# Small TensorE products of the token mixers put in another order: by the shape of their operands, two heads side by side

## The chip, the cores and the metric

The kernel runs on one core of a Trainium2 chip. A core has five engines that work side by side and wait for each other through semaphores: PE (TensorE: matrix products, with PEld for the load of the stationary operand), DVE (VectorE), ACT (ScalarE), POOL (GpSimd) and SP (SyncE, which here only issues DMAs). PE takes its work in the order of the program. The metric is the time of one execution on the device, in microseconds.

## What is computed

One step of a two-layer decoder for 16 meta tokens, 512 prompt tokens and 8 x 4 sample tokens (560 columns in all). Each layer adds a mixer and an MLP to the stream, each followed by a norm over 1024 features. The mixer consists of three causal token mixers on the same input: gated linear attention (GLA, 4 heads), Mamba-2 SSD (8 heads, 2 groups) and retention (4 heads). All three are the same recurrence, taken chunk by chunk:

```python
def step(s, inp):                       # one chunk: queries, keys, values, log-decays
    qc, kc, vc, gc = inp
    G = jnp.cumsum(gc, axis=1)
    ...
    o = (jnp.einsum('btsh,bshv->bthv', att, vc)
         + jnp.einsum('bthk,bhkv->bthv', qc * jnp.exp(G), s))
    s_new = (jnp.exp(G_end)[..., None] * s
             + jnp.einsum('bshk,bshv->bhkv', kc * jnp.exp(G_end[:, None] - G), vc))
    return s_new, o
```

An output is the sum of the chunk's own part (weights `att` by values) and of the part of the state that the chunk found (`q` by `s`); the new state adds keys by values. Around the mixers stand large products with the weights: the projections, three gated branch projections, an output projection and an MLP of 4096 hidden features. All results are fp32; the large products run as three products of operands split in two parts.

## The kernel before

The stream is kept feature-major: 128 features in the partitions, tokens in the columns. A **dense** tile is 128 output features for half of the tokens (256 to 288 columns), 24 products of 128x128 weights for an input of 1024 features, in one of three PSUM buffers named `dps`; ACT and DVE split each weight unit into its two parts (`wh`, `wl`) beside them.

The mixers and norms are written as generators, the **background**. `Background.slot` is called four times in each half tile; it adds a credit and, when the credit covers the distance that the last step left (`GAP`), emits the next step in the midst of the dense products. So all orders are fixed when the program is built, and nothing is moved at run time. The queue runs GLA, then SSD, then retention. `together` takes the steps of two generators in turn (one pair's heads beside the next pair's weights). A step may also leave small operations in `bg.soon`, which the following slots emit.

Small products use three PSUM buffers in rotation, `mps` (a bank each), and one of two banks, `sps`. An fp32 product is two passes on PE, so the profile counts two instructions for each.

`heads_gen` (L708) serves GLA and retention, a pair of heads at a time. It runs over four body chunks of 128 tokens (L771). `tokens(c)` (L739) transposes the values of both heads and the keys of a chunk (three transposes), and ACT copies them to `xt`. A chunk then has, for each head, the product of its weights (in `t4a` or `t4b`, all 128 rows) with the values, and onto the same sum the product of the queries (`QS`, 64 rows: head 0 in rows 0 to 63, head 1 in rows 64 to 127) with the state `St` (`S_h` in the profile). Both heads' new states (keys 128 rows, 64 columns) follow. DVE updates the state, ACT copies both outputs over the weights, and the transposes of the next chunk come last on PE.

`ssd` (L1109) takes all eight heads of a chunk at once: after its decays and scores, `out_of(0)` (L1206, L1212) multiplies the weights `E` (tile `t4a`) of heads 0 to 3 with the inputs (`v`), then come the product of `C` with the state `S_s` (64 rows, two groups), the new state (`vh` by `kt`, 64 columns), `out_of(4)` for heads 4 to 7 (L1228) and the transposes of the gate `z` (L1237). `E` of heads 0 to 3 is finished by DVE, that of heads 4 to 7 by POOL, in the step before. DVE then adds up the output `yt` and the state, POOL adds the skip part, DVE multiplies by `z`, ACT squares for the norm; the next chunk's second step transposes the normed output back (`last`).

In the profile most operations show the line of a helper: L304 is any product, L314 any transpose, L317, L326 and L329 are operations of DVE, POOL and ACT. So groups are told apart by their tiles.

Of the kernel before, what the change touches and what calls it, by code (L numbers as in the profile page):

```python
# [31 lines left out]
# weights: buffers for units as loaded, for split ones; units split at a time  # L32
NRAW, NSPLIT, AHEAD = 3, 3, 2
# tiles taken by halves of the tokens: the first ones of the MLP; taken whole before those: w_o, second product of the MLP
FIRST, WHOLE_O, WHOLE_2 = 8, 3, 3
# steps of row scales per slot; products that keep the clock up at the start, beside the first and the last norm
SOON = 3
WARM = 20, 12, 10
# credit of the mixers' and norms' steps per slot, by phase, and the steps' distances
# [9 lines left out]
# ---------------------------------------------------------------- constants of the shapes  # L49
def _const_tables():  # L50
    """Tables that depend on the shapes alone."""
# [66 lines left out]
# ---------------------------------------------------------------- weights: units of [128, 1024], in the order of use  # L118
# [24 lines left out]
def _lay_out(inp):  # L143
    """The inputs in the order in which the chip reads them."""
# [46 lines left out]
def _collect(r):  # L191
    """The chip's outputs in the reference's order and shapes."""
    y = r["y"].transpose(2, 1, 0).reshape(T - NMETA, D)
    cv = r["conv"].transpose(0, 3, 2, 1).reshape(DEPTH, 59, 768)
    cs = cv[:, 3:].reshape(DEPTH, NB, 7, 768)[:, :, 4:7]
    return (np.ascontiguousarray(y[:SEQ].reshape(1, SEQ, D)), np.ascontiguousarray(y[SEQ:].reshape(NB, NS, D)),
            r["state_gla_prompt"], r["state_gla_sample"], r["state_ssm_prompt"], r["state_ssm_sample"],
            np.ascontiguousarray(cv[:, None, 0:3]), np.ascontiguousarray(cs), r["state_ret_prompt"], r["state_ret_sample"])


def bc(ap, axis, n):
    """A view that repeats ap n times along a new axis."""
    u = ap.unsqueeze(axis)
    shape = list(u.shape)
    shape[axis] = n
    return u.to_broadcast(shape)
# [6 lines left out]
class Background:  # L213
    """Steps of the token mixers and norms, dealt out between the dense products."""
# [12 lines left out]
    def one(self):  # L227
        """the next step; it leaves its distance to the one after"""
        while self.q:
            try:  # L230
                self.wait = next(self.q[0]) or 1.0
                return True
            except StopIteration:
                self.q.pop(0)
        self.wait = 0.0
        return False

    def flush(self):
        """what is to come soon, at once"""
        while self.soon:  # L240
            self.soon.pop(0)()
# [19 lines left out]
def together(a, b):  # L261
    """Steps of two generators in turn, until both have ended."""
# [10 lines left out]
def decoder_step_kernel(ctx: ExitStack, tc: tile.TileContext, I, O):  # L273
# [13 lines left out]
    # ---------------------------------------------------------------- buffers  # L287
# [45 lines left out]
    # ---------------------------------------------------------------- input, constants  # L333
# [11 lines left out]
    def warm(n):  # L345
        """products of ones: the tensor engine's clock stays up while it waits"""
# [50 lines left out]
    def rsqrt(y, v, t, n_it=3):  # L397
        """y = v ** -0.5 for v > 0 (t: scratch), in steps"""
# [10 lines left out]
    # ---------------------------------------------------------------- weights, split exactly in two parts  # L409
# [4 lines left out]
    class Stream:  # L414
        """Units in the order of seq: loaded ahead, split ahead; a split unit lives until its last use in the plan."""
# [17 lines left out]
        def room(self, now):  # L433
            """whether no work from plan entry now on reads the next unit's buffer"""
# [8 lines left out]
        def ahead(self, now, most=1 << 30):  # L443
            """split as many units as there are buffers"""
            most = min(len(seq), most, self.n_split + AHEAD)
            while self.n_split < most and self.room(now):
# [4 lines left out]
                if seq[self.n_split][1] == "adt":  # L451
                    # both parts side by side, as one stationary operand
# [19 lines left out]
    # ---------------------------------------------------------------- plan of dense work  # L472
# [3 lines left out]
    def item(keys, emit, again=None, where=((None, 0),)):  # L476
        """work on the units keys, or on those of an earlier item again; where: for each split unit its slab (None: the
        ring) and the first plan entry at which that is free"""
# [13 lines left out]
    def twice(lst, between, side=1, tags=(), since=0):  # L492
        """(keys, emit) per output tile, the first half of all of them before the second; the last units of the first pass
        are the first of the second one, still split. side: so many tiles of a pass begin side by side, where its input
        has just been made. tags: slabs free from plan entry since on, for split units"""
# [25 lines left out]
    def tiles(lst, first=0, tags=(), since=0):  # L521
        """(keys, emit) per output tile; the first ones by halves"""
# [7 lines left out]
    def dense(ws, nk, c, xh, xl, spl, halves, evac, m=128, two=None):  # L530
        """One output tile: a unit of nk row tiles, columns c.. of each; three products per part of the tokens.
        two: the sums of a tile that has two units, by half"""
        w_of = [(a if len(a.shape) == 3 else a.rearrange("p (k c) -> p k c", k=nk))[:, :, c:c + m] for a in ws[0]]
        # products (part of the weights, part of x, row tile): what is made last comes last
# [44 lines left out]
    def silu2(out, p):  # L579
        """out = 2 silu(p)"""  # L580
# [5 lines left out]
    # ---------------------------------------------------------------- norm over features, columns of one half  # L586
    def norm_gen(sums, c0, n, wn, bn, l, last=False, alone=False, first=False):
        """X (pre-norm) -> X, XH, XL (normed); sums: addends of X's sum, of its squares'; last: X, sent out; alone: beside
        nothing else"""
# [3 lines left out]
        # sums over the features, token-major: a chunk of 128 tokens per column  # L593
# [21 lines left out]
        # every partition gets every token's scale and shift  # L615
# [7 lines left out]
        # w (x rs) + (w nm + b)  # L623
# [25 lines left out]
    def x_norm(c0, n, e):  # L649
        """the first norm, of the loaded X; e: engine of the plain sums"""  # L650
# [16 lines left out]
    class Acc:  # L667
        """sums over the features of one half, collected while its tiles are made; apart: the last tile's an addend apart"""
# [6 lines left out]
        def add(self, xo):  # L675
            """one tile more; not beside the other half's norm, which has more need of the engine"""
# [25 lines left out]
    # ---------------------------------------------------------------- linear attention: what GLA and retention share  # L702
    def row_scales(ss, eps, dim):
        """(ss / dim + eps) ** -0.5 and the steps to it"""
# [3 lines left out]
    def heads_gen(hp, v, QS, KH, att, attm, atts, decay, decay_s, l, nm, y, yscal):  # L708
        """Two heads from their weights att [s, h2, c, t]: outputs, states. QS, KH: decayed q, k [128 (h2 k), T]."""
# [6 lines left out]
        # meta and samples, token-major: rows (h2, 32)  # L716
# [22 lines left out]
        def tokens(c):  # L739
# [4 lines left out]
            transpose(p[:, 256:384], KH[:, c0:c0 + 128])  # L744
            vk = T4("xt", [128, 384])
# [3 lines left out]
        vk = tokens(0)  # L749
# [21 lines left out]
        for c in range(4):  # L771
            c0 = NMETA + 128 * c
            po = mps(), mps()
            for h2 in range(2):
                mm(po[h2][:, 0:128], att[:, h2, c], vk[:, sl(h2, 128)], start=True, stop=False)
                mm(po[h2][:, 0:128], QS[sl(h2), c0:c0 + 128], St[sl(h2)], start=False, stop=True)
# [10 lines left out]
            if c < 3:  # L787
                vk = tokens(c + 1)
            yield GAP["hc" + nm[0]]
        sp.dma_start(out=O[f"state_{nm}_prompt"][l, 0, 2 * hp:2 * hp + 2].rearrange("h k v -> (h k) v"), in_=St)  # L790
        # samples
# [53 lines left out]
    # ---------------------------------------------------------------- GLA  # L845
    def gla(l, B):
# [32 lines left out]
        def levels(hp, out):  # L879
# [32 lines left out]
            def small(Xs, Xt, n):  # L912
                """meta and samples; n: place of the level among 8, 4, 2, 1, diagonal"""
# [99 lines left out]
    # ---------------------------------------------------------------- retention  # L1013
# [47 lines left out]
    # ---------------------------------------------------------------- SSD  # L1061
    def ssd_tokens(l, B):
        """the inputs of step sizes and decays, token-major: body chunks 0..3, meta 4, samples 5 (twice, at rows 0 and 32)"""
# [45 lines left out]
    def ssd(l, B):  # L1109
# [3 lines left out]
        # decays from a chunk's start, to its end, over all of it  # L1113
# [30 lines left out]
        def steps(nt, ci, g):  # L1144
            """a of each token, at the columns from that token on"""
# [20 lines left out]
        for c, (c0, nt, ci) in enumerate(chunks):  # L1166
# [43 lines left out]
            if do_o:  # L1210
                po = mps()
                out_of(0)  # L1212
                yt, xd = T4("yt", [128, 512]), T4("sq", [128, 512])
# [13 lines left out]
            if do_o:  # L1227
                out_of(4)  # L1228
# [7 lines left out]
            if do_o:  # L1236
                pz = mps()  # L1237
                for i in range(4):
                    transpose(pz[0:nt, sl(i, 128)], z[:, i, cols])
# [16 lines left out]
        # samples: rows (g, token)  # L1256
# [93 lines left out]
        # columns (i, g, t) of p: feature tile 2 g + i  # L1350
# [4 lines left out]
    # ---------------------------------------------------------------- causal convolution of x, B, C  # L1355
# [39 lines left out]
    # ---------------------------------------------------------------- a layer  # L1395
    def layer(l):
        B = {}
        part = full if l == 0 else ((NMETA, HALF - NMETA), (HALF, T - HALF))
        # the last norm has nothing beside it: the smaller half comes last
# [30 lines left out]
        def split_y(br, nm):  # L1430
            """a mixer's output in two parts, where the one before has been used"""
# [30 lines left out]
        # retention's q, k are rotated one tile later than they are made  # L1462
# [29 lines left out]
        # gates and projections, branch by branch; then the normed x again, for the residual  # L1492
# [54 lines left out]
        # output projection, residual, first norm  # L1547
# [12 lines left out]
        def by_halves(tile_of, whole, wn, bn, tags=(), last=False):  # L1560
            """the last tiles half by half, so that one half's norm runs beside the other half's products"""
# [30 lines left out]
        # MLP in two halves of the hidden features  # L1592
# [87 lines left out]
```

## Time and profile before

| | us |
|---|---|
| median of 3 runs | 2128.74 (2128.52 to 2129.56) |
| span of the profiled execution | 2126.3 |
| PE busy in it | 2087.0 |
| DVE busy | 1119.0 |
| ACT busy | 745.8 |
| POOL busy | 519.8 |
| weights and state read, written | 171.46 MB, 9.67 MB |

The span runs from the first to the last instruction of the profiled execution; no other time of that execution is recorded, so it stands beside the median of the runs. A row of the timeline gives start, length, engine, line, the tile written, the tiles read, for a product the rows*columns of the stationary operand and the shape of the moving one, the number of instructions merged in the row, and in brackets idle time of that engine before it with what ended it. The first mixer's chunks of layer 0 lie at 174 to 280 us of the span, those of SSD at 325 to 400, of retention at 470 to 537; layer 1 has them at 1225 to 1327, 1374 to 1440 and 1512 to 1577.

### The profile page before, as it was taken

To read this page: it belongs to the slowest core of one execution; us is meant where nothing else is said; L and a number is where in the kernel's file an instruction comes from. 1 tells how busy PE (TensorE), PEld (TensorE's weight loads), DVE (VectorE), ACT (ScalarE), POOL (GpSimd) and SP (SyncE) were. 2 spreads that over 40 slices of the span, in tenths; PEclk is the share of its full clock that TensorE was granted. 3 is DMA by queue.
4 is the path that set the end of the run, shared out by engine and by line. 5 is a ranking of instruction groups with operands and counts; after the bars stand their busy time and mean duration, and the time that the engine had idled before them with its cause. 6 is when DMAs were issued, how large, how long until landed. Compare 5 with 4: busy or idle time off the path is not lost.

```text
span 2126.3 us, 39955 instructions
## 1 busy us (share of the span) xinstructions
PE 2087.0 (98%) x16536; PEld 1985.9 (93%) x16536; DVE 1119.0 (53%) x2206; ACT 745.8 (35%) x1373; POOL 519.8 (24%) x670
## 2 busy tenths in 40 slices
PE   8999999999999999999999999999999989999998
PEld 7998899888998999999999989988889989999998
DVE  8576567754556532333375774686544474223335
ACT  5434232222234531243254432322223354214433
POOL 4012114322334310021231121141323342001123
PEclk8999999999999999999999999999999999999999
DMA  4321321232222222222322223213222312222231
GB/s 158 103 80 67 96 86 51 80 92 72 81 91 89 71 89 90 80 90 81 120 101 93 80 71 108 83 54 96 71 72 90 102 68 100 90 90 80 92 128 63
DMA packets 87846, 186.00 MB, mean 87 GB/s; under 512 B 24624, under 2 KB 47216, under 8 KB 87664
## 3 DMA queue, kind: packets, MB, share of 16 engines
q1 hardware_dynamic: 87136, 182.86, 25.8%
q8 instruction: 130, 2.13, 0.4%
q10 hardware_dynamic: 528, 0.59, 0.1%
q14 instruction: 52, 0.43, 0.1%
HBM read 171.46 MB, written 9.67 MB: 85 GB/s over the span
## 4 chain that ended last, share of the span: by engine, by line
PE 86%; DVE 7%; issue 3%; POOL 2%; ACT 1%; DVEq 0%; POOLq 0%; ACTq 0%
PE dps L304 75%; PE mps L304 8%; PE sps L304 2%; PE mps L314 2%; DVE X L326 1%; POOL X L317 1%; DVE wl L317 1%; DVE XL L317 1%; POOL yt L317 0%; DVE xbc L326 0%; DVE S L317 0%; ACT wh L329 0%; POOL S L317 0%; ACT t4a L329 0%; DVE gv L317 0%
## 5 line engine op out<-in xcount | busy, mean ns | idle before, releaser
L304 PE MATMUL dps<-XH,wh 128*128 128x288 f32 (+2 forms) x2784 | 741.4, 296 | 7.1 <-ACT XH L329 6.9
L304 PE MATMUL dps<-XL,wh 128*128 128x288 f32 (+2 forms) x2784 | 727.8, 291 | 2.2 <-DVE XL L317 1.6
L304 PEld LDWEIGHTS dps<-XH,wh 128*128 128x128 f32 x2784 | 525.4, 189 | 21.4 <-ACT XH L329 9.6
L304 PEld LDWEIGHTS dps<-XL,wh 128*128 128x128 f32 x2784 | 524.3, 189 | 6.3 <-DVE XL L317 5.8
L317 DVE TENSOR_TENSOR wl<-raw,wh 128x1024 fp32r<-128x1024 f32 x278 | 345.2, 1243 | 212.3 <-ACT wh L329 197.2
L304 PE MATMUL dps<-XH,wl 128*128 128x288 f32 (+2 forms) x2752 | 429.7, 292 | 0.0
L329 ACT ACTIVATE wh<-raw 128x1024 fp32r<-128x1024 f32 x280 | 292.8, 1047 | 262.7 <-PE dps L304 227.3
L304 PEld LDWEIGHTS dps<-XH,wl 128*128 128x128 f32 x2752 | 380.5, 189 | 4.0 <-issue 2.7
L317 POOL TENSOR_TENSOR S<-th 128x288 f32<-128x288 f32 (+2 forms) x128 | 87.2, 682 | 499.2 <-ACT th L329 496.2
L304 PE MATMUL dps<-gqk,wh 128*128 128x288 f32 (+2 forms) x608 | 142.6, 295 | 1.6 <-ACT gqk L329 1.1
L329 ACT ACTIVATE th<-dps,parcol 128x288 f32<-128x288 f32 (+2 forms) x128 | 62.6, 489 | 187.8 <-PE dps L304 187.8
L304 PE MATMUL dps<-gqk,wl 128*128 128x272 f32 (+2 forms) x496 | 126.8, 292 | 0.0
L304 PE MATMUL dps<-Q,wh 128*128 128x288 f32 (+2 forms) x640 | 116.3, 291 | 0.8 <-ACT Q L329 0.8
L304 PEld LDWEIGHTS dps<-gqk,wh 128*128 128x128 f32 x608 | 104.1, 188 | 5.5 <-ACT gqk L329 2.8
L304 PE MATMUL dps<-gv,wh 128*128 128x288 f32 (+2 forms) x608 | 103.4, 291 | 0.0
L329 ACT ACTIVATE gt<-dps 128x272 f32<-128x272 f32 (+1 forms) x96 | 37.7, 398 | 173.8 <-PE dps L304 168.6
L304 PEld LDWEIGHTS dps<-Q,wh 128*128 128x128 f32 x640 | 96.8, 188 | 1.2 <-ACT Q L329 1.2
L317 DVE TENSOR_TENSOR X<-X,dps 128x288 f32<-128x288 f32 (+2 forms) x64 | 28.2, 441 | 130.1 <-PE dps L304 130.1
L317 POOL TENSOR_TENSOR X<-X,yt 128x288 f32<-128x288 f32 (+2 forms) x77 | 77.3, 1036 | 69.0 <-ACT yt L329 69.0
L304 PEld LDWEIGHTS dps<-gqk,wl 128*128 128x128 f32 x496 | 89.9, 188 | 2.9 <-issue 2.3
L317 POOL TENSOR_TENSOR X<-X,th 128x288 f32<-128x288 f32 (+2 forms) x56 | 47.8, 857 | 174.5 <-DVE th L326 174.4
L304 PEld LDWEIGHTS dps<-gv,wh 128*128 128x128 f32 x608 | 87.1, 188 | 0.4 <-DVE gv L317 0.3
(418 smaller groups left out, 3179.0 us busy)
## 6 DMA issues: line engine op xcount, KB each, us to landing
raw<-in_w SPq DMA_DIRECT2D x304, 512.0 KB, 3.3
craw<-Q SPq DMA_DIRECT2D x32, 70.0 KB, 2.0
S<-in_state_gla SPq DMA_DIRECT2D x8, 256.0 KB, 4.4
out_state_gla_sample<-S SPq DMA_DIRECT2D x8, 256.0 KB, 4.2
S<-in_state_ret SPq DMA_DIRECT2D x8, 256.0 KB, 3.8
out_state_ret_sample<-S SPq DMA_DIRECT2D x8, 256.0 KB, 2.5
S<-in_state_ssm SPq DMA_DIRECT2D x12, 128.0 KB, 3.1
out_state_ssm_sample<-S SPq DMA_DIRECT2D x12, 128.0 KB, 2.7
```

What stands on the lines that cost most here:

```text
L304: pe.matmul(out, lhsT=lhsT, rhs=rhs, start=start, stop=stop)
L314: pe.transpose(out, in_=in_, identity=ident[b:b + p, b:b + p])
L317: e.tensor_tensor(out=out, in0=a, in1=b, op=op)
L326: dve.scalar_tensor_tensor(out=out, in0=a, scalar=s, in1=b, op0=op0, op1=op1)
L329: act.activation(out=out, in_=in_, func=f, **k)
```

## The change

Three things are moved, and no operation is added or left out. In `heads_gen` the transposes of the next chunk go to the front of a chunk (their copy by ACT stays at its end), and the two heads' 128-row products come before their two 64-row products, which then stand next to each other. In `ssd`, `out_of(4)` follows `out_of(0)` at once, and the transposes of `z` follow that, ahead of the state's products. Comments are left out as well.

```diff
@@ heads_gen
-        def tokens(c):
+        def turned(c):
             c0 = NMETA + 128 * c
             p = mps()
             for h2 in range(2):
                 transpose(p[:, sl(h2, 128)], v[:, 2 * hp + h2, c0:c0 + 128])
             transpose(p[:, 256:384], KH[:, c0:c0 + 128])
+            return p
+
+        def tokens(p):
             vk = T4("xt", [128, 384])
             fn(vk, p[:, 0:384], AF.Copy)
             return vk
 
-        vk = tokens(0)
+        vk = tokens(turned(0))
@@
         for c in range(4):
             c0 = NMETA + 128 * c
+            pt = turned(c + 1) if c < 3 else None
             po = mps(), mps()
             for h2 in range(2):
                 mm(po[h2][:, 0:128], att[:, h2, c], vk[:, sl(h2, 128)], start=True, stop=False)
+            for h2 in range(2):
                 mm(po[h2][:, 0:128], QS[sl(h2), c0:c0 + 128], St[sl(h2)], start=False, stop=True)
...
             if c < 3:
-                vk = tokens(c + 1)
+                vk = tokens(pt)
@@ ssd
             if do_o:
                 po = mps()
                 out_of(0)
+                out_of(4)
+                pz = mps()
+                for i in range(4):
+                    transpose(pz[0:nt, sl(i, 128)], z[:, i, cols])
...
             if do_o:
-                out_of(4)
                 tt(dve, yt[0:nt], yt[0:nt] if c else xd[0:nt], po[0:nt], A)
...
             if do_o:
-                pz = mps()
-                for i in range(4):
-                    transpose(pz[0:nt, sl(i, 128)], z[:, i, cols])
                 stt(yt[0:nt], yt[0:nt], 0.5, pz[0:nt], M, M)
```

On PE, at the first chunk of GLA's first pair of heads in layer 0 (tiles: `t4a` the weights, `xt` the transposed values and keys, `X` the queries, `gv` the values; a row here is a product, its shape that of the moving operand):

```order
 L304 MATMUL dps<-XH,wl 128x288 x8
-L304 MATMUL mps<-xt,t4a 128x128
-L304 MATMUL mps<-S_h,X 128x128
-L304 MATMUL mps<-xt,t4a 128x128
-L304 MATMUL mps<-S_h,X 128x128
-L304 MATMUL mps<-xt 64x128 x2
 L314 MATMUL mps<-cst,gv 128x128 x2
 L314 MATMUL mps<-cst,X 128x128
+L304 MATMUL mps<-xt,t4a 128x128 x2
+L304 MATMUL mps<-S_h,X 128x128 x2
+L304 MATMUL mps<-xt 64x128 x2
 L304 MATMUL dps<-XH,wh 128x272
```

The three transposes now stand ahead of the chunk's products, and the products of one kind stand together.

On PE, at the first 128-token chunk of SSD in layer 0 (`v,t4a` the eight heads' weights by inputs, `S_s,xbc` the state product, `vh,kt` the new state, `cst,z` the transposes of the gate):

```order
 L304 MATMUL dps<-XH,wl 128x272 x2
-L304 MATMUL mps<-v,t4a 128x64 x4
+L304 MATMUL mps<-v,t4a 128x64 x8
+L314 MATMUL mps<-cst,z 128x128 x4
 L304 MATMUL sps<-S_s,xbc 128x256 x2
 L304 MATMUL mps<-vh,kt 64x256 x2
-L304 MATMUL mps<-v,t4a 128x64 x4
-L314 MATMUL mps<-cst,z 128x128 x4
 L304 MATMUL dps<-XH,wl 128x272 x6
```

The second four heads and the gate's transposes moved from the end of the block to its front half. The orders of ACT, DVE, POOL and SP are the same as before.

## The prediction, made before the changed kernel ran

> **What bounds the kernel now.** I read the page first: busy times, granted clock, chain.
>
> ```profile
> span 2126.3 us, 39955 instructions
> ...
> PE 2087.0 (98%) x16536; PEld 1985.9 (93%) x16536; DVE 1119.0 (53%) x2206; ACT 745.8 (35%) x1373; POOL 519.8 (24%) x670
> ...
> PEclk8999999999999999999999999999999999999999
> ...
> PE 86%; DVE 7%; issue 3%; POOL 2%; ACT 1%; DVEq 0%; POOLq 0%; ACTq 0%
> ```
>
> TensorE is busy for 98% of the span at full clock and carries 86% of the chain that ended last; the other engines are half idle. So a microsecond less of work on PE, in a stage where PE waits for nobody, is a microsecond off the end, and a new wait of PE is one more. "Busy" hides what matters here, though: it also covers drains between products of different shapes. For those I read the timeline of PE alone around one chunk of the linear-attention heads (start, length, then rows*columns of the stationary operand and the shape of the moving one).
>
> ```profile
> 181.19 0.29 PE L304 MATMUL dps<-XL,wh 128*128 128x288 f32 x1
> 181.32 0.38 PE L304 MATMUL mps<-xt,t4a 128*128 128x128 f32 x2
> 181.63 0.49 PE L304 MATMUL mps<-S_h,X 64*128 64x128 f32 x2
> 182.05 0.49 PE L304 MATMUL mps<-xt,t4a 128*128 128x128 f32 x2
> 182.47 0.49 PE L304 MATMUL mps<-S_h,X 64*128 64x128 f32 x2
> 182.88 0.44 PE L304 MATMUL mps<-xt 128*64 128x128 f32 x4
> 183.25 0.44 PE L314 MATMUL mps<-cst,gv 128*128 128x128 f32 x2
> 183.53 0.27 PE L314 MATMUL mps<-cst,X 128*128 128x128 f32 x1
> 183.55 0.38 PE L304 MATMUL dps<-XH,wh 128*128 128x288 f32 x1
> 183.77 0.29 PE L304 MATMUL dps<-XL,wh 128*128 128x288 f32 x1
> ```
>
> An fp32 product is two passes (x2 for one product). A dense pass follows the one before by 0.13 us (181.19 to 181.32), so the dense pass at 183.55 really begins at 183.77 - 0.13 = 183.64, and the chunk costs 183.64 - 181.32 = **2.32 us**. Three transposes stand 0.11 apart (183.53 to 183.64 is one). Wherever the shape changes, far more passes: two passes at 181.32 last 0.31 until the next row starts, which is 0.11 + a drain of 0.20; a row that follows a change takes 0.42, the drain, both passes and 0.11 of weight load that nothing covers now. A chunk has five changes: 128 to 64 rows, back, to 64 again, to 64 columns, back to 128*128. The last chunk of four has no transposes:
>
> ```profile
> 195.11 0.39 PE L304 MATMUL mps<-xt,t4a 128*128 128x128 f32 x2
> ...
> 196.68 0.44 PE L304 MATMUL mps<-xt 128*64 128x128 f32 x4
> 197.04 0.81 PE L304 MATMUL dps<-XH,wl 128*128 128x288 f32 x4
> ```
>
> Four dense passes end at 197.85; the first ended 3 x 0.13 earlier, at 197.46, and began 0.29 before, at 197.17. From 195.11 that is **2.05 us**, and the 64-column row costs 197.17 - 196.68 = 0.49 up to the next dense pass.
>
> **The heads' chunks, edit by edit.** There are 32 (2 layers, GLA and retention, 2 pairs of heads, 4 chunks); 24 have transposes. After the change: three transposes, four passes of the two 128-row products, the two 64-row products, the 64-column row. Two rows are needed that this chunk doesn't show. First, whether a transpose before a product drains:
>
> ```profile
> 366.51 0.71 PE L314 MATMUL mps<-cst,xbc 128*128 128x128 f32 x5
> ...
> 366.98 0.71 PE L304 MATMUL sps<-t4b,mgt_r 128*128 128x512 f32 x2
> ```
>
> Five transposes pass to a 128-row product after 0.47 us: below 5 x 0.11, so no drain. Bounds for this step: 0 by this row, 0.20 a chunk by the drain above (24 x 0.20 = 4.8 us); I take 0, since it is the same pair of kinds. Second, what two 64-row products cost when they stand together, on different halves of the rows. The SSD scores are such a pair:
>
> ```profile
> 355.05 0.60 PE L314 MATMUL mps<-cst,yt 128*128 128x128 f32 x4
> ...
> 355.58 0.49 PE L304 MATMUL mps<-xbc 64*128 64x128 f32 x4
> ```
>
> Four passes take 0.49, exactly what two passes of one head take in the heads' chunk (0.49 at 181.63). The two halves run at once. The pair here starts fresh sums; ours adds to sums begun by the 128-row products, each in a bank of its own. Bounds: 0 more, or four passes in a row instead of two, 2 x 0.11 = 0.22 (32 x 0.22 = 7.0 us); I take 0, the nearest row.
>
> The Trainium skill ("TensorE: Matmul & The Clock Gate", Part 3, "The mechanism") says matrix products start and end strictly in program order, without reordering. By that rule two passes of the first head would go before the second head's, which is the 0.22; the row above disagrees, four passes in the time of two.
>
> So the new chunk: seven passes without a change, the last starting after 6 x 0.11, plus the drain 0.20: 0.86. The pair, as any row after a change: 0.42. The 64-column row up to the dense pass: 0.49. Sum **1.77**, against 2.32: 0.55 saved, x24 = 13.2 us. Without transposes: 3 x 0.11 + 0.20 + 0.42 + 0.49 = **1.44** against 2.05: 0.61, x8 = 4.9 us. Together **-18.1 us**, in stages where PE isn't held up by others.
>
> What could take it back: the transposes for the next chunk now go first, so they wait for ACT to have emptied their PSUM buffer, and the products behind them for ACT's copy of this chunk's operands, which before had the same wait. ACT does this well ahead in most chunks; I put +0.2 us for the few that are close. DVE's state update and ACT's copies sit behind PE and get their sums a little earlier.
>
> **The SSD chunks.** Here the page's groups say little; the timeline of all engines does (chunk 2 of layer 0, PE's dense rows left out).
>
> ```profile
> 358.26 0.69 DVE L317 TENSOR_TENSOR t4a<-t4a,sm 128x512 f32<-128x512 f32 x1
> ...
> 359.10 1.08 PE L304 MATMUL mps<-v,t4a 128*128 128x64 f32 x8 [0.53 <-DVE t4a L317]
> ...
> 359.29 1.58 POOL L317 TENSOR_TENSOR t4a<-t4a,sm 128x512 f32<-128x512 f32 x1 [1.68 <-DVE sm L317]
> ...
> 360.10 0.70 PE L304 MATMUL sps<-S_s,xbc 64*128 64x256 f32 x4
> ...
> 360.73 0.65 PE L304 MATMUL mps<-vh,kt 128*64 128x256 f32 x4
> ...
> 361.32 1.11 PE L304 MATMUL mps<-v,t4a 128*128 128x64 f32 x8
> ...
> 361.69 0.68 DVE L317 TENSOR_TENSOR yt<-sps,eg 128x512 f32<-128x512 f32 x1
> ...
> 362.26 0.61 PE L314 MATMUL mps<-cst,z 128*128 128x128 f32 x4
> ```
>
> Before: heads 0 to 3, state product (64 rows), new state (64 columns), heads 4 to 7, transposes of z: three changes of shape. After: heads 0 to 7, z, state product, new state: again three (z to 64 rows, to 64 columns, back to dense). **By drains nothing is gained**, but for the 16-token chunk of layer 0, which has one change fewer: -0.2 us once.
>
> What moves is a wait. Heads 4 to 7 use weights that POOL finishes at 359.29 + 1.58 = 360.87. Before, PE got there at 361.32, with two other rows in between; now it comes straight after heads 0 to 3, whose group ends at 360.18, so the next pass could begin 0.17 earlier (the last pass began 0.28 before its end, the next comes 0.11 after that): 360.01. PE starts 0.15 after such a producer ends (DVE 358.95, PE 359.10), so at 361.02: **1.01 us of waiting**, with nothing to do, as PE takes its work in order. The other chunks, by the same sum:
>
> ```profile
> 342.24 1.56 POOL L317 TENSOR_TENSOR t4a<-t4a,sm 128x512 f32<-128x512 f32 x1 [1.62 <-DVE sm L317]
> ```
>
> ```profile
> 343.04 1.00 PE L304 MATMUL mps<-v,t4a 128*128 128x64 f32 x8
> ```
>
> ```profile
> 392.19 1.27 POOL L317 TENSOR_TENSOR t4a<-t4a,sm 128x512 f32<-128x512 f32 x1 [1.46 <-DVE sm L317]
> ```
>
> ```profile
> 392.38 1.00 PE L304 MATMUL mps<-v,t4a 128*128 128x64 f32 x8
> ```
>
> ```profile
> 1418.34 1.07 PE L304 MATMUL mps<-v,t4a 128*128 128x64 f32 x8 [0.27 <-DVE t4a L317]
> ...
> 1418.53 1.58 POOL L317 TENSOR_TENSOR t4a<-t4a,sm 128x512 f32<-128x512 f32 x1 [0.89 <-DVE sm L317]
> ```
>
> ```profile
> 1435.02 1.08 PE L304 MATMUL mps<-v,t4a 128*128 128x64 f32 x8
> ...
> 1435.22 1.27 POOL L317 TENSOR_TENSOR t4a<-t4a,sm 128x512 f32<-128x512 f32 x1 [1.30 <-DVE sm L317]
> ```
>
> The first chunk: 342.24 + 1.56 + 0.15 = 343.95 against 344.04 - 0.17 = 343.87: 0.08; I count the other layer's first alike. Four chunks (from 359.10 to 1418.34) have POOL starting 0.19 after PE: 1.02 each at the last of them. The fourth ones: 393.61 against 393.21, 0.40; 1436.64 against 1435.93, 0.71. Sum 0.16 + 4.1 + 1.1 = **+5.3 us**. Some comes back, as PE reaches two later waits of its own 1.0 us later while the work it waits for there isn't later by as much. The waits view has them:
>
> ```profile
> PE mps L314 <- DVE yt L321: 1.0, 2, 0.8
> ```
>
> I take all of it, **-1.0**; 0 is the other end. DVE now gets the state product after heads 4 to 7 and z, some 1.6 us later than at 361.69; I take this as covered by its idle time further on, and keep 4 chunks x 1.6 = 6.4 us as the end where it isn't.
>
> **Sum**: -18.1 + 0.2 - 0.2 + 5.3 - 1.0 = **-13.8 us**, so a span of 2112.5. The span of the profiled execution, 2126.3, lies 2.4 below the median of the runs, 2128.7; with that offset kept, 2128.7 - 13.8 = **2114.9 us**.
>
> **Rivals.**
> - The SSD wait costs nothing (POOL's work is nearer PE's need than I read): no 5.3, no 1.0: 2128.7 - 18.1 = 2110.6. Against it speak POOL rows that end 0.9 us after PE is ready. 0.14.
> - The pairs run in sequence: 2114.9 + 7.0 = 2121.9. The scores row speaks against it; that our pair adds to open sums speaks for it. 0.05.
> - The change doesn't do what it says, in that transposes and products drain between each other after all: + 4.8 = 2119.7. The five transposes speak against. 0.04.
> - DVE, held at the state product, hands on what stands behind it late (weight splits, emptied sums): up to + 6.4 = 2121.3. DVE's 53% speaks against. 0.09.
> - **Slower**: the reordered chunk start makes PE wait in every heads' chunk for ACT. ACT's weight split takes 1.05 us (292.8 us for 280, below); if one stands ahead of the copy that frees the buffer in each of 24 chunks, with no margin left, 24 x 1.05 = 25.2 and the time is 2140. It decides from 13.8 / 24 = 0.58 us a chunk. Against it: ACT is busy 35%, and PE waits for no such copy before. 0.03.
>
> ```profile
> L329 ACT ACTIVATE wh<-raw 128x1024 fp32r<-128x1024 f32 x280 | 292.8, 1047 | 262.7 <-PE dps L304 227.3
> ```
>
> **How the numbers follow.** My forecast has 0.65. Its own range is 2112.5 to 2117.5. All cases but the last are below the old time; a fifth of a per cent, 4.3 us, is what measurements can tell, and 2124.4 lies above every rival but the last. Faster 0.95, same 0.03, slower 0.02. The range takes in the cheap SSD case and most of the costly ones: 2109.5 to 2121.5.
>
> **What would show it.** Heads' chunks of 1.77 and 1.44 us, with the two 64-row products as one row x4 of 0.49. In SSD chunks a PE idle row before the later half of the group from t4a, put down to POOL, 1.0 in four chunks. No new wait of PE for ACT's xt or t4a. I am wrong if the 64-row row is still 0.42 a head, if a drain stands between transposes and products, or if PE's dense rows after an SSD chunk wait for DVE.

## The result, and the profile after

The changed kernel took **2117.43 us** (median of 4 runs, 2115.14 to 2118.79) against 2128.63 us for the kernel before, run beside it (4 runs, 2128.01 to 2129.56). The ratio is 0.9946, with a 95% interval of 0.9932 to 0.9960: the change is faster by 11.2 us. Forecast were 2114.9 us, 13.8 us less, in a range of 2109.5 to 2121.5; the median lies just inside the upper end of the forecast's own, narrower range (2112.5 to 2117.5).

The profiled execution of the changed kernel is the one of 2115.14 us, the fastest of the four. Its page, top lines and the granted clock:

```profile
span 2113.4 us, 39942 instructions
...
PE 2071.7 (98%) x16536; PEld 1975.9 (93%) x16536; DVE 1119.1 (53%) x2206; ACT 745.5 (35%) x1373; POOL 520.0 (25%) x670
...
PEclk8999999999999999999999999999999999999999
```

The span is 12.9 us shorter (2126.3 before), and PE's busy time fell by 15.3 us (2087.0 to 2071.7). That is the mark of this change: PE does the same products, 16536 instructions as before; drains went, and 15.3 - 12.9 = 2.4 us came back as idle time of PE.

The same heads' chunk as in the prediction, on PE's timeline of the changed kernel:

```profile
181.24 0.38 PE L314 MATMUL mps<-cst,gv 128*128 128x128 f32 x2
181.46 0.27 PE L314 MATMUL mps<-cst,X 128*128 128x128 f32 x1
181.57 0.61 PE L304 MATMUL mps<-xt,t4a 128*128 128x128 f32 x4
182.11 0.49 PE L304 MATMUL mps<-S_h,X 64*128 64x128 f32 x4
182.53 0.44 PE L304 MATMUL mps<-xt 128*64 128x128 f32 x4
182.90 0.40 PE L304 MATMUL dps<-XH,wh 128*128 128x288 f32 x1
183.13 0.29 PE L304 MATMUL dps<-XL,wh 128*128 128x288 f32 x1
```

The next dense pass begins at 183.13 - 0.13 = 183.00, so the chunk costs 183.00 - 181.24 = **1.76 us** (2.32 before). The three transposes pass to the products after 0.11 (181.46 to 181.57): no drain. The two heads' 64-row products are one row of four passes, 0.49 long, as two passes were before. And the last chunk of a pair of heads, without transposes:

```profile
193.93 0.61 PE L304 MATMUL mps<-xt,t4a 128*128 128x128 f32 x4
194.47 0.49 PE L304 MATMUL mps<-S_h,X 64*128 64x128 f32 x4
194.89 0.44 PE L304 MATMUL mps<-xt 128*64 128x128 f32 x4
195.26 1.06 PE L304 MATMUL dps<-XH,wl 128*128 128x288 f32 x6
196.16 0.29 PE L304 MATMUL dps<-XH,wh 128*128 128x272 f32 x1
```

The next tile's first pass begins at 196.16, six passes of 0.13 stand ahead of it, so the first of these begins at 195.37 and the chunk cost 195.37 - 193.93 = **1.44 us** (2.05 before).

Two chunks differ. The larger difference is at the first chunk of the first pair in layer 0, where the timeline has a wait between the two heads' products (PE's and DVE's rows):

```profile
174.27 0.39 PE L304 MATMUL mps<-xt,t4a 128*128 128x128 f32 x2
174.91 0.34 DVE L317 TENSOR_TENSOR attm<-mps,cst 16x16 f32<-16x16 f32 x2
175.30 0.49 PE L304 MATMUL mps<-xt,t4a 128*128 128x128 f32 x2 [0.65 <-DVE attm L317]
```

It costs 2.67 us in place of 1.76. `attm` is no operand of this product: it holds the meta tokens' weights of the next pair, and DVE fills it out of a PSUM buffer `mps`. With the transposes in front, the second head's product is the third to ask for an `mps` buffer after those scores, with three in rotation, so it gets theirs, and starts 0.05 after DVE has read it (174.91 + 0.34 = 175.25). Before, the third to ask were the transposes at the chunk's end. The other chunk, the second one of layer 1, costs 1.88: ACT's copy to `xt` ends there at 1226.80, and PE's row that reads it starts at 1226.85.

SSD's chunk 2 of layer 0, timeline of the changed kernel (PE's rows, and the two weights' producers that matter):

```profile
355.22 1.07 PE L304 MATMUL mps<-v,t4a 128*128 128x64 f32 x8 [0.46 <-DVE t4a L317]
355.42 1.58 POOL L317 TENSOR_TENSOR t4a<-t4a,sm 128x512 f32<-128x512 f32 x1 [1.68 <-DVE sm L317]
...
357.05 1.10 PE L304 MATMUL mps<-v,t4a 128*128 128x64 f32 x8 [0.76 <-POOL t4a L317]
357.99 0.61 PE L314 MATMUL mps<-cst,z 128*128 128x128 f32 x4
358.53 0.70 PE L304 MATMUL sps<-S_s,xbc 64*128 64x256 f32 x4
```

POOL ends the weights of heads 4 to 7 at 357.00, and PE starts on them at 357.05 after 0.76 us without anything to do. The view of PE's waits in the changed kernel (what it waited for: us in total, times, longest) shows this over all chunks, and the one of the first heads' chunk:

```profile
PE mps L304 <- POOL t4a L317: 3.5, 5, 0.8
...
PE mps L304 <- DVE attm L317: 0.6, 1, 0.6
```

Both are new. The row of before for DVE's `yt` (1.0 us, 2 times) is gone.

Summed over all blocks of small products, each measured as above from where the dense passes stop to where they go on, the two profiles compare like this:

| us | before | after | difference | forecast |
|---|---|---|---|---|
| heads' chunks with transposes, 24 | 24 x 2.317 | 22 x 1.763, 2.672, 1.882 | -12.3 | -13.2 + 0.2 |
| heads' chunks without, 8 | 8 x 2.04 | 8 x 1.437 | -4.8 | -4.9 |
| SSD, 128-token chunks, 8 | 30.2 | 35.3 | +5.05 | +5.3 |
| SSD, 16-token chunk of layer 0 | 2.205 | 2.310 | +0.1 | -0.2 |
| later blocks whose wait for `yt` went | 1.48, 2.03 | 1.12, 1.06 | -1.3 | -1.0 |
| sum | | | -13.3 | -13.8 |

The span fell by 12.9, and the 0.4 between the two is what remains of larger differences outside the changed chunks. One can be read at the same 24 dense passes, far from any chunk. Before:

```profile
704.72 0.39 PE L304 MATMUL dps<-XH,gqk 128*128 128x272 f32 x1 [1.91 <-ACT th L329]
...
707.85 0.29 PE L304 MATMUL dps<-XH,wh 128*128 128x288 f32 x1
```

And in the changed kernel, with a row of the view by windows (us; busy time and instructions of PE, PEld, DVE, ACT, POOL; then the granted clock, DMA share, GB/s):

```profile
698.08 0.39 PE L304 MATMUL dps<-XH,gqk 128*128 128x272 f32 x1 [1.92 <-ACT th L329]
...
702.72 0.29 PE L304 MATMUL dps<-XH,wh 128*128 128x288 f32 x1
```

```profile
698.40:701.80 3.40, 3.40 (x17) 3.40 (x16) 2.14 (x5) 2.14 (x6) 1.37 (x3) 0.50 0.02 5
```

The wait ahead of them is the same, but the passes took 702.72 - 698.08 = 4.64 us in place of 3.13, since the granted clock was halved. That is 1.5 us lost in this execution; at the start and the end of the program it is 1.1 us shorter than the profile before.

### The profile page after: what moved, and what is told of

The parts are those of the page before. It is cut to its first block, busy times and chain, and to the rows that moved or that the text cites. A ratio compares the mean times of both kernels' runs of the same rounds, so it can differ in the third digit from the quotient of the medians.

```text
span 2113.4 us, 39942 instructions
## 1 busy us (share of the span) xinstructions
PE 2071.7 (98%) x16536; PEld 1975.9 (93%) x16536; DVE 1119.1 (53%) x2206; ACT 745.5 (35%) x1373; POOL 520.0 (25%) x670
## 4 chain that ended last, share of the span: by engine, by line
PE 70%; DVE 4%; issue 2%; POOL 2%; ACT 1%; DVEq 0%; POOLq 0%; ACTq 0%
PE dps L304 63%; PE mps L304 5%; POOL X L317 1%; PE sps L304 1%; PE mps L314 1%; DVE X L326 1%; DVE wl L317 0%; DVE XL L317 0%; POOL S L317 0%; DVE gv L317 0%; DVE xbc L326 0%; ACT wh L329 0%; DVE th L326 0%; ACT t4a L329 0%; DVE X L317 0%
```

## The experiments

Two theories of the gain are apart by construction: it comes from the grouping by shape and the pair of 64-row products, or partly from the transposes at the front. And two of the loss: SSD's new order waits for POOL's weights (mine), or the wait is only shown there and something else would take its place. Each experiment gives the time of the kernel before on the same chip: 2128.59 us (median of 15 runs) for the first four, 2128.42 (15 runs) for the others.

**The heads' part alone** (label e1_heads_only): SSD's order put back, the rest of the change kept.

```diff
                 out_of(0)
-                out_of(4)
-                pz = mps()
-                for i in range(4):
-                    transpose(pz[0:nt, sl(i, 128)], z[:, i, cols])
...
+                out_of(4)
                 tt(dve, yt[0:nt], yt[0:nt] if c else xd[0:nt], po[0:nt], A)
...
+                pz = mps()
+                for i in range(4):
+                    transpose(pz[0:nt, sl(i, 128)], z[:, i, cols])
```

> SSD's part undone, the heads' part kept. If the SSD move is a loss through PE's wait for POOL's weights: span about 2109.6 (2113.4 less 3.8: the eight SSD blocks 5.05 us shorter, two later waits for DVE's yt 1.3 us longer, the 16-token block 0.1 shorter), time 2111 to 2114. Rival, the wait only took the place of drains and the block is neutral: span 2113 to 2114, time 2115 to 2119.

Measured: 2110.91 us (4 runs, 2110.70 to 2111.78), ratio 0.9917 [0.9904, 0.9931]. That is just under the expected range and 6.5 us below the changed kernel, whose nine runs in both sets lie at 2115.14 to 2118.79, so SSD's part is a loss. The profiled spans (2110.0 here) are only 3.4 apart, close to the 3.8 expected: the SSD blocks are 5.1 us shorter, and the two waits for `yt` cost 1.3 again. What makes up the rest of the 6.5 isn't shown; the changed kernel was profiled in its fastest execution, this one in its slowest of four. The timeline of this kernel at SSD's chunk 2:

```profile
356.27 1.58 POOL L317 TENSOR_TENSOR t4a<-t4a,sm 128x512 f32<-128x512 f32 x1 [1.68 <-DVE sm L317]
...
358.29 1.10 PE L304 MATMUL mps<-v,t4a 128*128 128x64 f32 x8
```

POOL ends at 357.85, and PE comes for the weights at 358.29, after the state's products: no idle time in brackets. The block takes 4.31 us again, as before.

**SSD's part alone** (e2_ssd_only): the heads' order put back.

```diff
-            pt = turned(c + 1) if c < 3 else None
...
-            for h2 in range(2):
                 mm(po[h2][:, 0:128], QS[sl(h2), c0:c0 + 128], St[sl(h2)], start=False, stop=True)
...
-                vk = tokens(pt)
+                vk = tokens(turned(c + 1))
```

> The heads' part undone, SSD's kept. If the SSD move is a loss: span about 2130 (2126.3 + 3.8), time 2131 to 2134, slower than before by 0.1 to 0.2%. Rival, it is neutral or gains by its sorting: 2126 to 2129.

Measured: 2132.55 us (11 runs, 2130.11 to 2135.21), ratio 1.0021 [1.0012, 1.0030]: slower than before by 4.0 us in the median, and by 6.4 us in the profiled span (2132.7). The profiled execution (2134.59) is among the slower ones, and its profile shows where the larger figure comes from. Its timeline at chunk 2, PE without the dense rows:

```profile
360.71 1.70 PE L304 MATMUL mps<-v,t4a 128*128 128x64 f32 x8 [0.75 <-POOL t4a L317]
362.20 1.06 PE L314 MATMUL mps<-cst,z 128*128 128x128 f32 x4
363.19 1.23 PE L304 MATMUL sps<-S_s,xbc 64*128 64x256 f32 x4
```

The wait is the same as in the changed kernel (0.75, 0.76 there), but behind it everything takes nearly twice as long: the transposes of `z` 1.06 in place of 0.61, the state product 1.23 in place of 0.70. The view by windows gives the reason. In this kernel:

```profile
361.00:364.40 3.40, 3.40 (x18) 2.42 (x17) 0.55 (x2) 0.00 (x0) 3.10 (x3) 0.51 0.02 5
364.40:367.80 3.40, 3.40 (x16) 2.64 (x15) 2.19 (x5) 0.00 (x0) 1.28 (x1) 0.50 0.00 0
```

And in the changed kernel, in a window at the same place in the program, 0.3 us behind the start of the same products:

```profile
357.35:360.75 3.40, 3.40 (x27) 2.52 (x26) 2.01 (x5) 0.00 (x0) 3.09 (x3) 1.00 0.02 5
```

PE is busy throughout in both, at half the clock in the one and at the full clock in the other. The block took 7.30 us in place of 5.25 (at half clock the dense passes stand 0.24 apart, 365.81 to 366.05, so the first of them begins 0.24 before the second).

**The pair alone** (e3_pairs_only): e1, and in addition the transposes back at the end of the chunk, so that only the two 64-row products stand together.

```diff
-            pt = turned(c + 1) if c < 3 else None
...
-                vk = tokens(pt)
+                vk = tokens(turned(c + 1))
```

> SSD's part undone; in the heads only the two 64-row products stand together, the transposes stay at the chunk's end as before. If a drain of 0.20 per change of shape and the side by side pair are all of the gain: a chunk with transposes has three changes as in the changed kernel and takes 1.71 us (0.33 + 0.20 + 0.42 + 0.37 + 0.39), and the wait of the first chunk of GLA (0.9) goes: span 1 to 2.5 us below e1, about 2107.5. Rival, putting the transposes ahead of the products is part of the gain: a chunk of 1.9 to 2.0 us, span 3 to 6 us above e1.

Measured: 2110.78 us (5 runs, 2109.89 to 2112.04), ratio 0.9916 [0.9903, 0.9930], span 2108.3. A chunk costs 1.716 us, 0.05 less than with the transposes in front; the first chunk of layer 0 has no wait (1.752), although DVE's `attm` comes as late as in the changed kernel:

```profile
174.07 0.60 PE L304 MATMUL mps<-xt,t4a 128*128 128x128 f32 x4
175.04 0.34 DVE L317 TENSOR_TENSOR attm<-mps,cst 16x16 f32<-16x16 f32 x2
```

Both heads' products are through before DVE starts, so they don't need `attm`; they need a free buffer, and here they have one. A second chunk in each layer has a wait for ACT's copy instead (2.155 and 2.187), as this kernel's timeline shows:

```profile
180.78 0.71 PE L304 MATMUL mps<-xt,t4a 128*128 128x128 f32 x4 [0.17 <-ACT xt L329]
```

The medians of e3 and e1 can't be told apart: the move of the transposes is worth nothing, and the pair is the whole gain.

**The weights of heads 4 to 7 on DVE** (e4_weights_dve): the changed kernel, with POOL's work that PE waits for given to DVE.

```diff
-            tt((dve, pool)[g], E...)
+            tt(dve, E...)
```

> The changed kernel, with the weights of heads 4 to 7 multiplied on DVE in place of POOL (0.69 us after those of heads 0 to 3, in place of POOL's 1.58 which start later). If PE's wait for POOL is what the SSD move costs: SSD blocks fall from 3.6 to 5.25 us to 3.5 to 4.2, no idle of PE put down to POOL t4a, span about 2109 to 2111. Rival, the block is held by something else (DVE's queue, a PSUM bank): spans 2112.5 to 2115, blocks as in the changed kernel.

Measured: 2116.26 us (5 runs, 2115.96 to 2118.64), ratio 0.9944 [0.9931, 0.9956], span 2114.5: no gain over the changed kernel. The expectation (a span of 2109 to 2111) missed, and its rival, DVE's queue, holds. The timeline of chunk 3 in layer 0:

```profile
372.62 1.08 PE L304 MATMUL mps<-v,t4a 128*128 128x64 f32 x8 [0.84 <-DVE t4a L317]
372.71 1.21 DVE L317 TENSOR_TENSOR t4a<-t4a,sm 128x512 f32<-128x512 f32 x1
...
373.97 1.11 PE L304 MATMUL mps<-v,t4a 128*128 128x64 f32 x8 [0.28 <-DVE t4a L317]
```

And the row of its view of waits that stands in place of POOL's:

```profile
PE mps L304 <- DVE t4a L317: 3.2, 6, 1.0
```

The wait for POOL is gone, and DVE's own queue makes PE wait as long: 3.2 us in 6 waits, where it was 0.6 in 2 in the changed kernel. In chunk 3 PE now waits 0.84 for the first half of the weights, and the second half takes DVE 1.21. The clock was halved here too, from 375.2 to 378.6 us, and the block took 6.37 us.

**The transposes alone** (e5_transposes_only): e1 with the loop over the two heads' products joined again, so that only the transposes are in front.

```diff
             for h2 in range(2):
                 mm(po[h2][:, 0:128], att[:, h2, c], vk[:, sl(h2, 128)], start=True, stop=False)
-            for h2 in range(2):
                 mm(po[h2][:, 0:128], QS[sl(h2), c0:c0 + 128], St[sl(h2)], start=False, stop=True)
```

> SSD's part undone; in the heads only the transposes go to the chunk's front, each head's 64-row product again follows its 128-row product. If changes of shape are the cost, a chunk keeps five of them (the one from the 64-column products to the transposes becomes one to the dense products): 2.3 us as before, the first GLA chunk 0.9 longer, span 2126 to 2128, time as before within 0.1%. Rival, the place of the transposes is part of the gain: chunks of 1.9 to 2.1 us, span 2118 to 2122.

Measured: 2129.82 us (11 runs, 2128.45 to 2131.22), ratio 1.0007 [0.9998, 1.0015]: no change, as expected. A chunk costs 2.367 us, 0.05 more than before, with both 64-row products again as rows of their own on PE's timeline:

```profile
182.27 0.49 PE L304 MATMUL mps<-S_h,X 64*128 64x128 f32 x2
182.69 0.49 PE L304 MATMUL mps<-xt,t4a 128*128 128x128 f32 x2
183.10 0.48 PE L304 MATMUL mps<-S_h,X 64*128 64x128 f32 x2
```

The transposes go in front without a drain, and no change of shape goes away with them.

**`z` between the halves** (e7_z_between): the changed kernel, with the transposes of `z` ahead of heads 4 to 7 as cover of POOL's work. This is the test of the wait that e4 failed to be, since it takes nothing from another engine's queue.

```diff
                 out_of(0)
-                out_of(4)
                 pz = mps()
                 for i in range(4):
                     transpose(pz[0:nt, sl(i, 128)], z[:, i, cols])
+                out_of(4)
```

> The changed kernel with the transposes of z between heads 0 to 3 and heads 4 to 7, in place of behind them: same products, same three changes of shape, but 0.45 us more of work ahead of the wait. If the wait for POOL is the cost: four SSD blocks fall from 4.7 to 5.25 us to 4.3 to 4.8, all eight by 2 to 3 us in sum, span about 2111 (where the clock isn't halved there), time 2112.5 to 2115. Rival, something later in the block holds it: sums as in the changed kernel.

Measured: 2114.07 us (5 runs, 2113.46 to 2114.55), ratio 0.9932 [0.9919, 0.9946], span 2111.7. Timeline at chunk 2, and the row of the waits:

```profile
356.29 1.58 POOL L317 TENSOR_TENSOR t4a<-t4a,sm 128x512 f32<-128x512 f32 x1 [1.68 <-DVE sm L317]
...
357.93 1.10 PE L304 MATMUL mps<-v,t4a 128*128 128x64 f32 x8 [0.31 <-POOL t4a L317]
```

```profile
PE mps L304 <- POOL t4a L317: 1.3, 4, 0.3
```

Half a microsecond of cover takes the wait from 0.76 to 0.31, over all chunks from 3.5 to 1.3 us. The eight SSD blocks take 33.0 us in place of 35.3; 0.8 of that comes back at the two later waits for `yt` (1.58 and 1.43 us in place of 1.12 and 1.06). The difference of the spans, 1.7, isn't a measure of it, since the two profiles also differ in the clock far from SSD: the 1.5 us at 698 us of the changed kernel aren't lost here. The runs are the better measure: nine of the changed kernel all lie above the five of this one.

**The changed kernel again** (r1_after_again), unaltered, for a second profile.

> The changed kernel again, for its spread and another profile. If its longer executions are those in which the new waits in SSD halve PE's granted clock for a stretch of 3.4 us or more, as in the run with the SSD part alone: an execution of 2117 or more shows a clock of 0.5 between 320 and 440 or 1360 and 1480 us of the span, one of 2115 doesn't; times 2115 to 2119, spread over 2.5 us, where the kernels without the SSD part spread over 1 to 2. Rival, the spread is that of the norms or of DMA: the same spread in kernels without the SSD part, the clock in SSD full.

Measured: 2116.97 us (5 runs, 2115.55 to 2117.79), ratio 0.9945 [0.9933, 0.9958]. The profiled execution took 2116.76 us, with a span of 2115.0, 1.6 us more than the first. PE's timeline at chunk 3:

```profile
375.30 1.11 PE L304 MATMUL mps<-v,t4a 128*128 128x64 f32 x8 [0.75 <-POOL t4a L317]
376.25 1.03 PE L314 MATMUL mps<-cst,z 128*128 128x128 f32 x4
377.21 1.23 PE L304 MATMUL sps<-S_s,xbc 64*128 64x256 f32 x4
```

The view by windows there:

```profile
376.30:379.70 3.40, 3.40 (x14) 1.66 (x14) 1.22 (x3) 0.00 (x0) 2.40 (x3) 0.50 0.00 0
```

The same program, with the same wait of 0.75, has the half clock for 3.4 us here and had none at this place in its first profile. The block took 6.54 us in place of 4.98, 1.56 more; chunk 4 gives 0.35 back (3.59 in place of 3.93), so the SSD blocks are 1.2 us longer. That is most of the 1.6 us between the two spans; the program's first 60 us hold 0.7 more, and small differences go the other way. The expectation that kernels without SSD's part spread less, over 1 to 2 us, didn't hold: e3 spreads by 2.2, e6 by 2.3, e5 by 2.8 and the kernel before by 3.8, against 2.2 here.

**State product beside the scores** (e6_state_with_scores): e3, and SSD regrouped in another way. The 64-row state product goes to the 64-row products of the scores, one step earlier; `z` follows heads 0 to 3, and heads 4 to 7 come last, behind the new state.

```diff
+                if c:
+                    pst = sps()
+                    for g in range(2):
+                        mm(pst[:, g, 0:256], xbc[sl(g), 5, cols], S_s[sl(g)].rearrange("p h d -> p (h d)"))
...
                 out_of(0)
-                out_of(4)
                 pz = mps()
...
-                    p2 = sps()
-                    for g in range(2):
-                        mm(p2[:, g, 0:256], xbc[sl(g), 5, cols], S_s[sl(g)].rearrange("p h d -> p (h d)"))
...
+                out_of(4)
```

> The heads as in e3 (64-row products together, transposes last); in SSD the 64-row product with the state goes one step earlier, behind the 64-row scores, and the transposes of z follow heads 0 to 3, with heads 4 to 7 last. By the theory of drains SSD blocks lose one change of shape: each loses the row of 0.63 us and the scores' block gains about 0.43 (two passes of 256 columns side by side), 1.6 us in all, with no new wait for POOL: span 1 to 2 us below e3's 2108.3, time 2108.5 to 2110. Rival, the state isn't ready at the scores or DVE is later for it: as e3 or above.

Measured: 2110.38 us (4 runs, 2108.75 to 2111.06), ratio 0.9914 [0.9900, 0.9927], span 2106.9. Six of the eight SSD blocks take 2.955 us, 0.58 less than the least before; the scores' block takes 0.43 more, since the state product there costs no change of shape, as PE's timeline shows:

```profile
351.69 0.49 PE L304 MATMUL mps<-xbc 64*128 64x128 f32 x4
352.02 0.60 PE L304 MATMUL sps<-S_s,xbc 64*128 64x256 f32 x4
```

Some of it is given back at a later wait, that for `yt`, which the shorter blocks leave less covered, 2.0 us in place of 1.0 before; its row in the view of waits:

```profile
PE mps L314 <- DVE yt L321: 2.0, 2, 1.3
```

The span is 1.4 below e3's, as expected; the median lies above the 2108.5 to 2110 that were expected. This is the lowest median measured, and it beats the kernel before and the changed one; from e1 and e3 it can't be told apart.

## Why the prediction was right, and where its sizes were off

**The bound and the direction: right.** Drains of PE were removed where nothing else held PE up, and e3 shows the whole gain with the pair alone: 2128.59 - 2110.78 = 17.8 us.

**The heads' chunks: right in mechanism and in size.** 1.77 and 1.44 us were forecast; 1.763 and 1.437 were measured, in 30 of 32 chunks. The two bounds that I had set at nothing held: transposes pass to products without a drain (0.11 from one row to the next, and e5 changes nothing), and the two 64-row products run at once, onto sums already begun too.

On the latter the prediction weighed a rule of the Trainium skill ("TensorE: Matmul & The Clock Gate", Part 3, "The mechanism") that products start and end in program order, and read it as two passes more. That reading was too strong. The same section describes products on different rows of the array that start one after the other and overlap, so order and overlap go together; the row of four passes in 0.49 us agrees with that.

**The +0.2 us for waits at chunk starts: mis-sized.** It was +1.0: 0.91 in the first chunk of layer 0 and 0.12 in one of layer 1. I looked for ACT's copies, and of those only the 0.12 for `xt` came. The larger one is a wait for a PSUM buffer, as the prediction had in mind, but another than it named: I thought of the transposes and of ACT. By going first, the transposes push every later product of the chunk one place on in the rotation of three, and the second head's product meets a buffer that DVE hasn't read yet. e3 shows that it hangs on where the transposes stand: with them at the end this wait goes, and waits for ACT's `xt` come in its place, which lengthen the second chunks of the two layers by 0.44 and 0.47.

**SSD: right in mechanism and in its sum.** +5.3 was forecast for the eight chunks and +5.05 measured, e1 takes it away by putting the order back, and e7 takes away a part of it by half a microsecond of cover. In chunk 2 I was slightly high (1.01 us, against 5.25 - 4.31 = 0.94): I gave PE 0.15 us from the end of its producer, and it took 0.05 (357.00 to 357.05). "By drains nothing is gained" held in the long chunks.

**The 16-token chunk: -0.2 forecast, +0.1 measured.** The count of changes of shape gave one drain fewer, and that was wrong. The timelines show that before, `z` passed to the dense passes without a drain (four transposes in 0.44 us, 330.15 to 330.59). After, the two groups of heads joined save 0.10, but `z` ahead of the new state takes 0.54, and the new state ahead of the dense passes 0.69 in place of 0.58.

**The recovery at later waits: -1.0 forecast, -1.3 measured,** and the row of the wait is gone as foreseen; e1, e3 and e7, where PE comes earlier, have it again.

**The step from the span to the median: a term without a reason, and luck.** The span came out at 2113.4, 0.9 above the forecast of 2112.5, with 1.5 us of it lost to the clock at 698 us. The median is 2.5 above its own forecast, 2117.43 against 2114.9. I had carried over the offset of the kernel before, 2.4 us, as if it belonged to the program. It doesn't: in every execution whose span and time are both on record the time is 1.7 to 1.9 us above the span. The rest of an offset only says where the profiled execution lies among the others, and here it was the fastest, 2.3 below the median.

What spreads the executions is open. The halved clock behind the new wait is one part: r1 has it in SSD and the first profile doesn't. But each of the ten profiles, that of the kernel before too, also has two to four stretches of 3.4 us at half clock between 670 and 705 us and between 1700 and 1751 us, far from any changed chunk, and not the same ones in each. The spread of 2 to 4 us in kernels without the SSD wait (e3, e5, e6, the kernel before) may come from these, and how much of the 2.5 us the new wait explains isn't shown.

**The rivals.** That the SSD wait costs nothing is out by e1 (SSD blocks 5.1 us shorter without it). Pairs in series and drains at the transposes are out by the rows at 181.24 to 182.53. DVE late at the state product: PE's wait for `yt` went away rather than grew. A wait for ACT in every chunk: it came in one, with 0.12 us.

## What to carry to other kernels

Where small products interrupt dense ones, count the changes of operand shape and put 64-row products of two heads, on different halves of the rows, next to each other: that was 0.55 to 0.60 us in each of 32 chunks here. Before moving a product forward, ask which independent products between it and its producer cover that producer's last microsecond; here regrouping without a drain to save moved only the cover, at 5 us in the SSD chunks. Ask the same of the buffer that it writes: who used it last, and is that done? Giving the late operand to another engine moved the wait into that engine's queue; other work of PE in between covered it, in part (e7) or whole (e1).

## What the runs showed of the hardware that wasn't expected

The granted clock is 1.00 or 0.50 in every trace, and it changes only at points that lie whole multiples of 3.413 us apart, to within 0.001 us (worked out from the clock's own records in each of the ten traces). The Trainium skill ("TensorE: Matmul & The Clock Gate", Part 1, "What's actually happening") has the clock halve after at least one idle window of about 3.4 us, a window that runs freely and doesn't start with the kernel. The length agrees, and so does that one execution has a half clock where another of the same program has none.

The trigger differs: no PE idle time of 3.4 us stands ahead of the stretches in SSD. In the four profiles in which PE waits for the heads' weights there (the changed kernel twice, e2, e4) 14 such waits lasted 0.75 to 0.97 us; three were followed by half the clock, for 3.4 us (e4 and r1) or twice that (e2). Waits for `yt` of 0.78 (before, e1, e3, e5) and 1.27 us (e6) were not. Nor does PE's busy time in one window decide. These two windows stand at the same place in the program, e2 and then the changed kernel, and each begins at one of those points:

```profile
357.60:361.00 3.40, 2.19 (x18) 1.85 (x16) 3.37 (x6) 0.00 (x0) 1.92 (x2) 1.00 0.38 145
```

```profile
353.60:357.00 3.40, 2.23 (x18) 1.90 (x16) 3.37 (x6) 0.00 (x0) 1.72 (x3) 1.00 0.47 154
```

They hold nearly the same work; the first was followed by the half clock, the second by the full one. What a window must hold isn't settled by these runs.
